# Empty places between the links of the ordered mixer's chains, and a second values block ahead of the second attention keys

## The chip, the cores and the metric

The kernel runs on one core of one Trainium2 chip. The metric is the device time of one execution in microseconds; the lower the better. TensorE is called PE here, VectorE DVE, ScalarE ACT, GpSimd POOL and SyncE SP, as the profile calls them.

## The reference

One decoder layer over 256 positions of width 2048: a feed-forward half step, a mixer of two groups of heads, a second feed-forward half step, each followed by a layer norm with a scaled residual.

```
x <- LN1(alpha*x + 0.5*SwiGLU_1(x))
x <- LN2(alpha*x + W_out [DiffAttn(x) || RWKV7(x)])
x <- LN3(alpha*x + 0.5*SwiGLU_2(x))
```

The mixer matters here. One projection `w_in` gives the columns of both kinds of heads. Differential attention has 8 heads with two softmaxes each: p = softmax(q1 k1) - lam * softmax(q2 k2), o = p v, then a norm over the head. RWKV7 has 16 heads of size 64, and its state goes from one position to the next:

```
sa    = einsum('bhvk,bhk->bhv', state, -kk_t)
state = state * w_t + sa * (kk_t * a_t) + v_t * k_t
y_t   = einsum('bhvk,bhk->bhv', state, r_t)
```

after a shift by one position, a decay w and a rate a from two low-rank products ("lora"), and a normalised kk. y goes through a group norm, gets a bonus from r, k and v, and is multiplied by a gate g. Both results go through `W_out`.

## The kernel before

**The weight stream.** Every weight comes from HBM once, in float32. A block of 512 columns takes 8 steps of 256 rows each. One step (`Stream.block`) loads 512 KB with a DMA on SP's queue (L130), ACT rounds it into `wh` (L140), DVE writes the rest, `wl` = raw - `wh` (L143), and PE forms two times six matmuls of 128x512: hi x wh (L150), hi x wl (L151), lo x wh (L152), for the first 128 positions of this step and for the second 128 of the step two back. In the mixer there are five pairs of `wh` and `wl`, so the pair of a step is used again five steps later, and three buffers for the raw weights.

**The chains as background.** At the end of each step `run_bg` goes over the generators that were spawned and lets each advance by one place: it calls `next` until the generator yields something other than 0. So `yield 0.6` (or any number but 0) ends a place, `yield 0` goes on in the same place, and `yield None` waits for a condition and asks again in the next place. `hold` skips a generator for some places. Below, place n is the n-th step after the one in which the lora block's results are turned (L575 for the first time).

**What the order is made of.** The mixer's part up to the last `stream.flush` runs under `manual_schedule` for PE: PE executes in the order in which the program is written. The order on DVE, ACT and POOL is set by a scheduler. Their instructions run in that order, so a DMA that ACT issues, or an operation that waits, holds up what is queued behind it there.

The blocks of `w_in` in this part: the lora block (8 steps), then twelve blocks of 8 steps: r1 (k, r, v of RWKV group 1), a1's q and k, r2's k and r, v1 (attention's first values), a2's q and k, r2's v, v2. When a block is finished, `chan_major` (L569 copies on ACT, L575 transposes on PE, one place later) or a copy hands it to the chains. Here r1, r2 are the two groups of eight RWKV heads (g = 0 and 1 in the code), a1, a2 the two groups of four attention heads.

**The RWKV chain of a group**, `rwkv_group`: L735 multiplies the lora result by its second matrix into the banks `pr` and `sm`, L739 puts a sigmoid on it (ACT), L743 sums the decays (DVE). When k is there, L749 to L752 prepare kk on DVE and ACT, L757 sums its squares over a head (PE), L758 to L774 scale everything on DVE and ACT. When r is there, L783 scales it; L793 forms the products of all positions of a chunk (PE, into `sm` and `pr`), L796 masks them into `Q` (DVE). Then `dU` and `U` go through HBM by DMAs from ACT's queue (L823, L826), L834 and L836 eliminate, 31 pairs of operations on DVE over 16 places, and the inverse goes back by more such DMAs (L840, L841 write `dY` and `dYT`, L848 and L852 read them). L860 and L871 finish the inverse; L811 turns `BK`; the four chunks c follow, links L890, L902 to L912, L921 and the output. After the last chunk L951 and L961 do the group norm, and L981 the gate. The second group waits with L793 until the first one's chunks are done ("chain").

**`rwkv_values`** turns v (L705, L712) and forms the bonus (`rk` at L699, L719).

**Attention**, `attn_heads`, two generators per group with two heads each: scores L1039 (PE, into `at` and `pr`), bias L1041 and maximum L1044, L1045 (DVE), exponentials L1049 (ACT), combination L1051 to L1055 (DVE), transposes L1060 and their copy L1062, product with v L1072, norm L1081 to L1096 (ACT, DVE and POOL), transposes L1100 and copy L1101.

Of the kernel before, what the change touches and what calls it, by code (L numbers as in the profile page):

```python
# [10 lines left out]
F32 = mybir.dt.float32  # L11
# [5 lines left out]
P = 128  # L17
D = 2048
S = 256
# [18 lines left out]
def build(tc, A, out):  # L38
# [58 lines left out]
    class Stream:  # L97
# [184 lines left out]

        def spawn(self, gen):
            self.bg.append(gen)

# [262 lines left out]
    def mix(mp, pq, C):  # L548
# [140 lines left out]
        def merge(x):  # L689
            return x.rearrange("p a c t -> p (a c) t")  # L690

        def rwkv_values(g, st):
            gr, prev = st["group"], st["prev"]
            while "fed" not in st or (prev is not None and "chain" not in prev):
                yield None
            vp, vv = gr.vp, gr.vv
            rk = t4("lw") if g == 0 else mp.tile([P, 4, S], F32, tag="vv", name=nm("rk"))
            for p in range(4):
                V.scalar_tensor_tensor(out=v4(rk)[:, p], in0=gr.rh[:, p], scalar=col(4, g, p), in1=gr.ka[:, p], op0=ALU.mult, op1=ALU.mult)  # L699
            SV = hp.tile([P, 4, 4, 2, 64], F32, tag="J1", name=nm("SV"))  # L700
            st["SV"] = SV
            for p in range(4):
                ps = bank(("pr", "sm")[p % 2], (P, 4, P))
                for c in range(4):
                    T.transpose(ps[:, c, :], vp[:, p, c * 64:c * 64 + P], ident)  # L705
                SC.copy(out=SV[64:128, p, :, 0, :], in_=ps[64:128, :, 0:64])
                SC.copy(out=SV[0:64, p, 0:3, 1, :], in_=ps[0:64, 1:4, 64:128])
                if p % 2 == 1:
                    yield 0.3
            ps = bank("pr", (P, 4, P))  # L710
            for p in range(4):
                T.transpose(ps[0:64, p, :], vv[:, p, 192:256], ident)  # L712
            SC.copy(out=SV[0:64, :, 3, 1, :], in_=ps[0:64, :, 64:128])
            st["turned"] = True
            yield 0.3
            for hf in range(2):
                ps = bank(("pr", "sm")[hf], (P, 2, S))
                for p in range(2):
                    T.matmul(ps[:, p, :], C["bones"], rk[:, 2 * hf + p, :], start=True, stop=True)  # L719
                V.tensor_tensor(out=vv[:, 2 * hf:2 * hf + 2, :], in0=ps, in1=vv[:, 2 * hf:2 * hf + 2, :], op=ALU.mult)  # L720
            yield 0.6
            st["values"] = True

        def rwkv_group(g, st):
# [5 lines left out]
            while "tw" not in lora:  # L730
                yield None
            for k in range(2):
                ps = [bank(t, (P, 2, S)) for t in ("pr", "sm")]
                for p in range(4):
                    T.matmul(ps[p // 2][:, p % 2, :], wa[:, p * P:(p + 1) * P], lora["tw"][:, k, :], start=True, stop=True)  # L735
                for p in range(4):
                    x = ps[p // 2][:, p % 2, :]
                    o, x = (tl[:, p, :], x) if k == 0 else (av[:, p], x.rearrange("p (c t) -> p c t", c=4))
                    SC.activation(out=o, in_=x, func=AF.Sigmoid, bias=col(k, g, p))  # L739
                yield 0.6  # L740
# [7 lines left out]
            for p in range(4):  # L748
                V.tensor_scalar(out=al[:, p], in0=ka[:, p], scalar1=col(2, g, p), scalar2=-1.0, op0=ALU.mult, op1=ALU.mult)  # L749
            SC.activation(out=v4(tl), in_=al, func=AF.Square)  # L750
            for p in range(4):
                V.tensor_scalar(out=be[:, p], in0=av[:, p], scalar1=-1.0, scalar2=col(3, g, p), op0=ALU.add, op1=ALU.mult)  # L752
# [9 lines left out]
            V.scalar_tensor_tensor(out=merge(ka), in0=merge(be), scalar=1.0, in1=merge(ka), op0=ALU.add, op1=ALU.mult)  # L762
            yield 1.1
            V.tensor_tensor(out=merge(al), in0=merge(al), in1=merge(v4(tl)), op=ALU.mult)
            yield 1.1

            SC.activation(out=tl, in_=cum, func=AF.Exp, scale=LDEC)
            SC.activation(out=cum, in_=cum, func=AF.Exp, scale=-LDEC)
            V.scalar_tensor_tensor(out=merge(av), in0=merge(av), scalar=-1.0, in1=merge(al), op0=ALU.mult, op1=ALU.mult)
            yield 1.1  # L770
# [12 lines left out]
            V.tensor_tensor(out=merge(rh), in0=merge(rh), in1=merge(v4(cum)), op=ALU.mult)  # L783
            yield 1.1
            while prev is not None and "chain" not in prev:
                yield None
# [13 lines left out]
            def transposed():  # L800
# [5 lines left out]
                for h in range(2):  # L806
                    for e in range(2):
                        r = slice(64 * e, 64 * e + 64)
                        ps = bank("sm", (P, 6, 64))
                        for i in range(6):  # L810
                            T.transpose(ps[:, i, :], BK[r, 2 * h + i // 3, i % 3, e:e + 2].rearrange("p a t -> p (a t)"), ident[r, r])  # L811
                        for p in range(2):
                            SC.copy(out=bt[2 * h + p][:, 0:3, e, :], in_=ps[:, 3 * p:3 * p + 3])
# [143 lines left out]
            for hf in range(2):  # L957
# [4 lines left out]
                SC.activation(out=merge(nrm[:, h2]), in_=merge(v4(ps)), func=AF.Ln, scale=1.0 / 64, bias=C["ge"])  # L962
                yield 0.6 * hf
            SC.activation(out=merge(nrm), in_=merge(nrm), func=AF.Exp, scale=-0.5)
            yield 0
# [7 lines left out]
            st["gate"] = True  # L973
            yield 0.6 * (1 - g)
            o = (hp, mp)[g].tile([P, 4, S], F32, tag=("H3", "vvd")[g], name=nm("og"))
# [25 lines left out]

        def attn_cols(g):
            st = {"q": qq[:, g]}

            def qkdone(tt, acc, n):
# [5 lines left out]
                def then():  # L1011
                    if n == "k":
                        st["left"] = 2
                        st["gens"] = [attn_heads(g, st, (i, i + 2)) for i in range(2)]
                        for i, x in enumerate(st["gens"]):
                            stream.spawn(x)
                            stream.hold[x] = i

                chan_major(acc, tt, [P] * 4, dst, then)

            stream.block(w_in, g * NB, NB, KX, x_lhs, lambda tt, acc: qkdone(tt, acc, "q"))
            stream.block(w_in, AW + g * NB, NB, KX, x_lhs, lambda tt, acc: qkdone(tt, acc, "k"))
            return st

        def attn_heads(g, st, heads):
            q, k = st["q"], st["k"]
            W = 3 * P
            spans = [slice(0, P), slice(P, W)]
            for h in heads:
# [23 lines left out]
                for qb in range(2):  # L1053
                    V.tensor_scalar(out=s[:, 0, spans[qb]], in0=s[:, 0, spans[qb]], scalar1=rr[:, qb, 0:1], scalar2=None, op0=ALU.mult)
                    V.scalar_tensor_tensor(out=s[:, 0, spans[qb]], in0=s[:, 1, spans[qb]], scalar=rr[:, qb, 1:2],  # L1055
                                           in1=s[:, 0, spans[qb]], op0=ALU.mult, op1=ALU.add)
                yield 0.6
                tr = bank("at", (P, 4, P))
# [6 lines left out]
                while "v" not in st:  # L1065
                    yield None
                if wait and heads[0] == 1:
                    yield 0.6
                vt = st["v"]
# [25 lines left out]
                for qb in range(2):  # L1095
                    V.tensor_scalar(out=ot[:, qb, :], in0=po[:, qb, :], scalar1=rs[:, 0, qb:qb + 1], scalar2=None, op0=ALU.mult)  # L1096
                yield 0.6
                tr = bank("at", (P, 4, P))
# [18 lines left out]
        attn_values(0, a1)  # L1117
        a2 = attn_cols(1)
        rwkv_cols(1, r2, (2,))
        attn_values(1, a2)  # L1120
# [137 lines left out]
```

## Time and profile before

| | |
|---|---|
| median of 3 runs | 1970.33 us (1967.61 to 1971.26) |
| the profiled execution's own time | 1970.74 us |
| its span in the trace | 1969.0 us |
| mean granted clock of TensorE | 0.983 |
| first FFN | up to about 706 us of the span |
| the mixer | about 706 to 1262 us |
| bytes read from HBM | 368.29 MB |

The profile is one execution, so its span (first to last instruction) and its own time are compared with each other, and the median of the runs with other medians. Where the text says "the mixer's window" it means 735 to 1131 us of the span, in which the chains named above run beside the stream. In the profile a row of a group gives how often an operation ran, its busy time, the mean ns of one, and the idle time of its engine just ahead of it with what ended it. A row of the table of waits gives which PE line waited for which instruction, how long in all, how often, and the longest.

### The profile page before, as it was taken

To read this page: it belongs to the slowest core of one execution; us is meant where nothing else is said; L and a number is where in the kernel's file an instruction comes from. 1 tells how busy PE (TensorE), PEld (TensorE's weight loads), DVE (VectorE), ACT (ScalarE), POOL (GpSimd) and SP (SyncE) were. 2 spreads that over 40 slices of the span, in tenths; PEclk is the share of its full clock that TensorE was granted. 3 is DMA by queue.
4 is the path that set the end of the run, shared out by engine and by line. 5 is a ranking of instruction groups with operands and counts; after the bars stand their busy time and mean duration, and the time that the engine had idled before them with its cause. 6 is when DMAs were issued, how large, how long until landed. Compare 5 with 4: busy or idle time off the path is not lost. (4 is left out here: it accounts for less than half of the span.)

```text
span 1969.0 us, 24893 instructions
## 1 busy us (share of the span) xinstructions
PE 1895.0 (96%) x9319; PEld 1554.9 (79%) x9319; DVE 1620.6 (82%) x1826; ACT 1094.9 (56%) x1376; POOL 73.0 (4%) x110
## 2 busy tenths in 40 slices
PE   9999999999999988889789999999999999999997
PEld 7788888888888877677667778788888888888886
DVE  7999988789998775586568676899999868899986
ACT  5656655556665545445444554366666555666652
POOL 0000101000000000000000000000000100000000
PEclk9999999999999999999899999999999999999999
DMA  8756676666666563445334546596556686556744
GB/s 298 247 201 223 192 240 225 223 210 219 204 201 207 163 193 107 139 137 152 97 110 145 150 138 206 191 309 221 182 193 203 226 276 214 182 193 215 226 164 133
DMA packets 207320, 381.72 MB, mean 194 GB/s; under 512 B 23530, under 2 KB 25648, under 8 KB 206944
## 3 DMA queue, kind: packets, MB, share of 16 engines
q1 hardware_dynamic: 182928, 350.53, 54.2%
q0 software_dynamic: 6832, 15.32, 2.9%
q10 hardware_dynamic: 17440, 14.29, 2.5%
q8 instruction: 73, 1.20, 0.2%
q14 instruction: 47, 0.39, 0.1%
HBM read 368.29 MB, written 11.80 MB: 193 GB/s over the span
## 5 line engine op out<-in xcount | busy, mean ns | idle before, releaser
L140 ACT CAST wh<-raw 128x1024 fp32r<-128x1024 f32 (+2 forms) x833 | 853.1, 1047 | 660.5 <-PE acc L152 437.0
L143 DVE TENSOR_TENSOR wl<-raw,wh 128x1024 fp32r<-128x1024 f32 (+2 forms) x833 | 983.4, 1213 | 230.8 <-ACT wh L140 226.3
L150 PE MATMUL acc<-wh,xh 128*128 128x512 f32 (+1 forms) x1552 | 612.0, 400 | 1.8 <-ACT xh L87 1.0
L151 PE MATMUL acc<-wl,xh 128*128 128x512 f32 (+1 forms) x1552 | 608.5, 393 | 2.1 <-DVE wl L143 2.0
L152 PE MATMUL acc<-wh,xl 128*128 128x512 f32 (+1 forms) x1552 | 607.4, 392 | 0.4 <-DVE xl L88 0.4
L150 PEld LDWEIGHTS acc<-wh,xh 128*128 128x128 f32 x1552 | 295.6, 191 | 65.6 <-issue 2.4
L152 PEld LDWEIGHTS acc<-wh,xl 128*128 128x128 f32 x1552 | 294.9, 190 | 62.3 <-DVE xl L88 1.1
L151 PEld LDWEIGHTS acc<-wl,xh 128*128 128x128 f32 x1552 | 295.4, 190 | 61.4 <-DVE wl L143 3.4
L221 DVE TENSOR_TENSOR raw<-raw,raw 128x2048 f32<-128x2048 f32 x112 | 255.8, 2284 | 2.3 <-DMA raw<-in_ffn_w_up_dram 1.0
L151 PE MATMUL acc<-wl,hh 128*128 128x512 f32 x544 | 212.0, 390 | 0.0
L152 PE MATMUL acc<-wh,hh 128*128 128x512 f32 x544 | 211.4, 389 | 0.0
L150 PE MATMUL acc<-wh,hh 128*128 128x512 f32 x544 | 210.9, 390 | 0.0
L150 PE MATMUL acc<-wh,s 128*128 128x512 f32 x448 | 174.9, 390 | 2.1 <-ACT wh L140 1.1
L152 PE MATMUL acc<-wh,s 128*128 128x512 f32 x448 | 174.6, 390 | 0.0
L151 PE MATMUL acc<-wl,s 128*128 128x512 f32 x448 | 174.4, 389 | 0.0
L150 PEld LDWEIGHTS acc<-wh,hh 128*128 128x128 f32 x544 | 102.1, 188 | 21.7 <-ACT wh L140 0.4
L152 PEld LDWEIGHTS acc<-wh,hh 128*128 128x128 f32 x544 | 102.1, 188 | 21.1
L151 PEld LDWEIGHTS acc<-wl,hh 128*128 128x128 f32 x544 | 102.1, 188 | 20.9
L150 PEld LDWEIGHTS acc<-wh,s 128*128 128x128 f32 x448 | 84.1, 188 | 20.3 <-ACT wh L140 1.5
L152 PEld LDWEIGHTS acc<-wh,s 128*128 128x128 f32 x448 | 84.1, 188 | 17.5
L151 PEld LDWEIGHTS acc<-wl,s 128*128 128x128 f32 x448 | 84.1, 188 | 17.4
L234 ACT COPY acc<-acc 128x512 f32<-128x512 f32 x28 | 16.0, 571 | 51.3 <-PE acc L152 47.5
(287 smaller groups left out, 1105.9 us busy)
## 6 DMA issues: line engine op xcount, KB each, us to landing
raw<-in_ffn_w_up_dram SPq DMA_DIRECT2D x176, 512.0 KB, 5.4
raw<-in_ffn_w_down_dram SPq DMA_DIRECT2D x176, 512.0 KB, 5.2
raw<-in_ffn_w_gate_dram SPq DMA_DIRECT2D x175, 512.0 KB, 4.6
raw<-in_w_in_dram SPq DMA_DIRECT2D x96, 512.0 KB, 3.6
raw<-in_w_out_dram SPq DMA_DIRECT2D x32, 512.0 KB, 3.8
sd<-s POOLq DMA_DIRECT2D x16, 256.0 KB, 4.0
s<-sd POOLq DMA_DIRECT2D x16, 256.0 KB, 4.9
xs<-y ACTq DMA_DIRECT2D x16, 256.0 KB, 2.7
```

Of the source, the lines that this page charges most:

```text
L140: SC.copy(out=wh[:, c, :w], in_=raw[:, c, :w])
L143: self.cut = V.tensor_tensor(out=wl[:, c, :w], in0=raw[:, c, :w], in1=wh[:, c, :w].bitcast(F32), op=ALU.subtract).ins
L150: T.matmul(a, hi, wh[:, j, :w], start=first and j == 0, stop=False, skip_group_check=True)
L151: T.matmul(a, hi, wl[:, j, :w], start=False, stop=False, skip_group_check=True)
L152: i = T.matmul(a, lo, wh[:, j, :w], start=False, stop=last and j == 1, skip_group_check=True)
L221: V.tensor_tensor(out=out, in0=x, in1=y, op=ALU.subtract)
L234: SC.copy(out=u, in_=a)
```

## The change

`rest(n)` is a generator that yields n places. The change puts it into the chains and moves some of their instructions:

- RWKV group: two empty places ahead of L735 in the first group; three ahead of L752; after L762 one in the first group (as before) and two in the second; one more ahead of L769 in the second group; three after L783 instead of one.
- The second group's L793 waits for the first group's norm ("normed") instead of the end of its chunks ("chain"), and the first group's gate (L981) waits until the second group's L793 are issued ("fed").
- L811 of the second group uses the bank `pr` for half of its transposes.
- Values: three empty places ahead of L705, one more ahead of L719; `rk` is formed after L712.
- Attention: an empty place ahead of the first head; the second pair of heads is held two places instead of one; in the first group two places instead of one ahead of L1060 and L1100; after the wait for v four places in the second pair of the first group (one in the second group). The first group's heads stand first in the background list.
- The second RWKV group's v block comes ahead of the second attention keys block, and behind the queries block.

```
+        def rest(n):
+            for i in range(n):
+                yield 0.6
...
-            rk = t4("lw") if g == 0 else mp.tile([P, 4, S], F32, tag="vv", name=nm("rk"))
-            for p in range(4):
-                V.scalar_tensor_tensor(out=v4(rk)[:, p], in0=gr.rh[:, p], scalar=col(4, g, p), in1=gr.ka[:, p], op0=ALU.mult, op1=ALU.mult)
+            yield from rest(3)
...
             while "tw" not in lora:
                 yield None
+            yield from rest(2 * (1 - g))
...
             SC.activation(out=v4(tl), in_=al, func=AF.Square)
+            yield from rest(3)
...
             V.tensor_tensor(out=merge(rh), in0=merge(rh), in1=merge(v4(cum)), op=ALU.mult)
-            yield 1.1
-            while prev is not None and "chain" not in prev:
+            yield from rest(3)
+            while prev is not None and "normed" not in prev:
                 yield None
...
-                        ps = bank("sm", (P, 6, 64))
+                        ps = bank(("sm", "pr")[e * g], (P, 6, 64))
...
+            st["normed"] = True
...
-            yield 0.6 * (1 - g)
+            while g == 0 and "fed" not in st["next"]:
+                yield None
...
-                            stream.spawn(x)
-                            stream.hold[x] = i
+                            stream.spawn(x, (i, None)[g])
+                            stream.hold[x] = 2 * i
...
             stream.block(w_in, g * NB, NB, KX, x_lhs, lambda tt, acc: qkdone(tt, acc, "q"))
+            between()
             stream.block(w_in, AW + g * NB, NB, KX, x_lhs, lambda tt, acc: qkdone(tt, acc, "k"))
...
-                yield 0.6
+                yield from rest(2 - g)
                 tr = bank("at", (P, 4, P))
...
-                if wait and heads[0] == 1:
-                    yield 0.6
+                if wait:
+                    yield from rest((1 + 3 * (1 - g)) * heads[0])
...
-        a2 = attn_cols(1)
-        rwkv_cols(1, r2, (2,))
+        a2 = attn_cols(1, lambda: rwkv_cols(1, r2, (2,)))
```

The changed kernel has a few more lines, so its lines count higher: L735 is L742 there, L752 is L760, L783 is L792, L793 is L802, L796 is L805, L834 and L836 are L843 and L845, L840 and L841 are L849 and L850, L848 and L852 are L857 and L861, L985 is L996, L1009 is L1020, L1049 is L1062, L1101 is L1114.

On the engines the instructions move as follows. First PE at place 25, where the second group's lora product stands. Before, the transposes of a block (L575) come ahead of it, and the stream follows:

```order
L150 MATMUL acc_6441<-wh_6559,xh_5804 128x512
L151 MATMUL acc_6441<-wl_6560,xh_5804 128x512
L152 MATMUL acc_6441<-wh_6559,xl_5805 128x512
L575 MATMUL tr_6643<-ident,tm_6599 128x128 x4
L735 MATMUL pr_6659<-tw,qq 128x256 x2
L735 MATMUL sm_6660<-tw,qq 128x256 x2
L150 MATMUL acc_6630<-wh_6671,xh_5678 128x512
L151 MATMUL acc_6630<-wl_6672,xh_5678 128x512
```

In the changed kernel the same place (L802 is L793 of before, L742 is L735):

```order
L802 MATMUL sm_6635<-AR_5962,BK_5963 128x128
L802 MATMUL pr_6636<-AR_5962,BK_5963 128x128
L742 MATMUL pr_6647<-tw,qq 128x256 x2
L742 MATMUL sm_6648<-tw,qq 128x256 x2
L150 MATMUL acc_6570<-wh_6659,xh_5689 128x512
L151 MATMUL acc_6570<-wl_6660,xh_5689 128x512
```

The first group's products have moved from places 19 to 22 to places 24 to 27, and stand right ahead of the second group's lora product, in the same two banks.

Second, ACT where the first group's inverse goes out and comes back (`dY`, `dYT`, `TT`, `YT`). Before:

```order
L1009 COPY qq<-tr_6998 128x4x128
L840 DMA dY_6608<-Y_6616 64x1024
L841 DMA dYT_6609<-U_6614 32x1024
L140 CAST wh_7084<-raw_7082 128x1024
L848 DMA TT_7158<-dY_6608 32x16x32 x4
L852 DMA YT_7164<-dYT_6609 32x16x32
L140 CAST wh_7108<-raw_7106 128x1024
L852 DMA YT_7164<-dYT_6609 32x16x32
L140 CAST wh_7134<-raw_7132 128x1024
```

In the changed kernel:

```order
L140 CAST wh_7306<-raw_7304 128x1024
L849 DMA dY_6759<-Y_6767 64x1024
L850 DMA dYT_6760<-U_6765 32x1024
L857 DMA TT_7294<-dY_6759 32x16x32 x3
L1062 ACT_TABLE_LOAD
L1062 ACTIVATE s_7209,ssum_7211<-s_7209,mx_7210 128x128 x2
L1062 ACTIVATE s_7209,ssum_7211<-s_7209,mx_7210 128x256 x2
L857 DMA TT_7294<-dY_6759 32x16x32
L861 DMA YT_7300<-dYT_6760 32x16x32 x2
L140 CAST wh_7327<-raw_7325 128x1024
```

No cast of the weight stream stands between the issues any more, and the exponentials of the first attention head (L1062) stand among them.

Third, DVE at the second group's elimination. Before, its first operations are spread between subtractions of the stream (L143):

```order
L143 TENSOR_TENSOR wl_8240<-raw_8237,wh_8239 128x1024
L834 TENSOR_TENSOR itmp_8192<-U_8168,Y_8170 64x31
L143 TENSOR_TENSOR wl_8288<-raw_8285,wh_8287 128x1024
L836 TENSOR_TENSOR Y_8170<-Y_8170,itmp_8192 64x31
L834 TENSOR_TENSOR itmp_8195<-U_8168,Y_8170 64x60
L836 TENSOR_TENSOR Y_8170<-Y_8170,itmp_8195 64x30x2
L143 TENSOR_TENSOR wl_8326<-raw_8323,wh_8325 128x1024
L834 TENSOR_TENSOR itmp_8217<-U_8168,Y_8170 64x87
```

In the changed kernel (L843 and L845 are L834 and L836; `og` is the first group's gated output, `qq` a finished head of attention):

```order
L143 TENSOR_TENSOR wl_8493<-raw_8490,wh_8492 128x1024
L843 TENSOR_TENSOR itmp_8402<-U_8352,Y_8354 64x60
L996 TENSOR_TENSOR og_8392<-BK_5963,sm_8393 128x512
L845 TENSOR_TENSOR Y_8354<-Y_8354,itmp_8402 64x30x2
L843 TENSOR_TENSOR itmp_8435<-U_8352,Y_8354 64x87
L845 TENSOR_TENSOR Y_8354<-Y_8354,itmp_8435 64x29x3
L843 TENSOR_TENSOR itmp_8438<-U_8352,Y_8354 64x112
L845 TENSOR_TENSOR Y_8354<-Y_8354,itmp_8438 64x28x4
L843 TENSOR_TENSOR itmp_8484<-U_8352,Y_8354 64x135
L1114 TENSOR_SCALAR qq<-at_8425,ng 128x256
L845 TENSOR_TENSOR Y_8354<-Y_8354,itmp_8484 64x27x5
L843 TENSOR_TENSOR itmp_8487<-U_8352,Y_8354 64x156
```

More of the elimination's operations stand in a row between two subtractions than before.

More of the change, by code (lines that the diff above doesn't have):

```diff
@@ L281, in flush, with spawn @@
                 self.puts.pop(0)[1]()
-        def spawn(self, gen):
-            self.bg.append(gen)
+        def spawn(self, gen, at=None):
+            self.bg.insert(len(self.bg) if at is None else at, gen)
         def put(self, f):
@@ L714, in rwkv_values @@
             st["turned"] = True
+            rk = t4("lw") if g == 0 else mp.tile([P, 4, S], F32, tag="vv", name=nm("rk"))
+            for p in range(4):
+                V.scalar_tensor_tensor(out=v4(rk)[:, p], in0=gr.rh[:, p], scalar=col(4, g, p), in1=gr.ka[:, p], op0=ALU.mult, op1=ALU.mult)
             yield 0.3
+            yield 0.6
             for hf in range(2):
@@ L762, in rwkv_group @@
             V.scalar_tensor_tensor(out=merge(ka), in0=merge(be), scalar=1.0, in1=merge(ka), op0=ALU.add, op1=ALU.mult)
-            yield 1.1
+            yield from rest(1 + g)
             V.tensor_tensor(out=merge(al), in0=merge(al), in1=merge(v4(tl)), op=ALU.mult)
@@ L768, in rwkv_group @@
             SC.activation(out=cum, in_=cum, func=AF.Exp, scale=-LDEC)
+            yield from rest(g)
             V.scalar_tensor_tensor(out=merge(av), in0=merge(av), scalar=-1.0, in1=merge(al), op0=ALU.mult, op1=ALU.mult)
@@ L783, in rwkv_group @@
             V.tensor_tensor(out=merge(rh), in0=merge(rh), in1=merge(v4(cum)), op=ALU.mult)
-            yield 1.1
-            while prev is not None and "chain" not in prev:
+            yield from rest(3)
+            while prev is not None and "normed" not in prev:
                 yield None
@@ L1000, in attn_values, with attn_cols @@
             stream.block(w_in, 2 * AW + g * NB, NB, KX, x_lhs, vdone)
-        def attn_cols(g):
+        def attn_cols(g, between=lambda: None):
             st = {"q": qq[:, g]}
@@ L1025, in attn_heads @@
         def attn_heads(g, st, heads):
+            yield 0.6
             q, k = st["q"], st["k"]
@@ L1096, in attn_heads @@
                     V.tensor_scalar(out=ot[:, qb, :], in0=po[:, qb, :], scalar1=rs[:, 0, qb:qb + 1], scalar2=None, op0=ALU.mult)
-                yield 0.6
+                yield from rest(2 - g)
                 tr = bank("at", (P, 4, P))
```

## The prediction

> **What bounds the kernel now.** I read the page first. Its rows for the span and for the engines put TensorE (PE) far ahead of the rest:
>
> ```profile
> span 1969.0 us, 24893 instructions
> PE 1895.0 (96%) x9319; PEld 1554.9 (79%) x9319; DVE 1620.6 (82%) x1826; ACT 1094.9 (56%) x1376; POOL 73.0 (4%) x110
> ```
>
> The mean hides stages, so next the table by stretches; its columns are length, then PE, PEld, DVE, ACT and POOL busy, the granted clock, the DMA share and GB/s. The first row lies in the first FFN, the second is the ordered mixer up to the 1131st us, the third is what follows it:
>
> ```profile
> 100.00:700.00 600.00, 599.51 (x2685) 496.69 (x2684) 527.25 (x477) 352.85 (x388) 26.78 (x40) 1.00 0.63 207
> 735.00:1131.00 396.00, 350.26 (x2104) 279.44 (x2105) 256.09 (x477) 194.58 (x327) 6.81 (x7) 0.94 0.45 131
> 1131.00:1250.00 119.00, 117.60 (x792) 95.18 (x791) 83.46 (x154) 58.41 (x112) 5.70 (x7) 1.00 0.54 176
> ```
>
> The FFN has no idle PE to win. The ordered mixer has 396.00 - 350.26 = 45.7 us of it, and its clock stands at 0.94; behind it another 1.4 us lie idle. What PE waits for in the second stretch, from the table of waits (in all, times, longest):
>
> ```profile
> PE pr L757 <- ACT tl L750: 9.9, 2, 5.3
> PE pr L705 <- DVE vv L591: 9.0, 2, 6.7
> PE sm L793 <- DVE AR L783: 5.7, 1, 5.7
> PE sm L890 <- DVE SV L921: 5.2, 1, 5.2
> PE at L1100 <- DVE ot L1096: 4.5, 2, 4.2
> PE pr L735 <- ACT tw L615: 3.7, 1, 3.7
> PE sm L981 <- DVE Q L796: 2.3, 1, 2.3
> PE acc L151 <- DVE wl L143: 1.5, 2, 0.8
> ```
>
> Nearly all of it is a link of a chain that stands in PE's row before its input is ready, not the weight stream (the last row, 1.5 us). The timeline around the third row shows how a link costs (start, length, engine, line):
>
> ```profile
> 800.29 0.39 PE L150 MATMUL acc<-wh,xh 128*128 128x512 f32 x1
> 800.52 0.39 PE L151 MATMUL acc<-wl,xh 128*128 128x512 f32 x1
> ...
> 802.80 1.23 DVE L143 TENSOR_TENSOR wl<-raw,wh 128x1024 fp32r<-128x1024 f32 x1 [0.45 <-ACT wh L140]
> ...
> 805.52 1.23 DVE L783 TENSOR_TENSOR AR<-AR,cum 128x1024 f32<-128x1024 f32 x1
> ...
> 806.80 2.08 PE L793 MATMUL sm<-AR,BK 64*128 64x128 f32 x16 [5.66 <-DVE AR L783]
> ...
> 810.25 0.63 PE L150 MATMUL acc<-wh,xh 128*128 128x512 f32 x1
> 810.68 0.63 PE L151 MATMUL acc<-wl,xh 128*128 128x512 f32 x1
> ```
>
> DVE serves weights and link in turn, PE stands for 5.66 us, and after it the matmuls come every 0.43 us instead of every 0.23. The windows of half clock that follow such gaps, three of the nine and the sum of all nine:
>
> ```profile
> 805.79:812.62 6.83, 5.82 (x25) 4.83 (x26) 3.93 (x8) 0.00 (x0) 0.00 (x0) 0.50 0.17 62
> 996.94:1000.35 3.41, 3.41 (x21) 2.54 (x19) 3.41 (x7) 0.00 (x0) 0.00 (x0) 0.50 0.51 157
> 1116.40:1119.81 3.41, 3.08 (x11) 2.54 (x12) 1.68 (x4) 1.52 (x3) 0.00 (x0) 0.50 0.89 304
> sum 51.21, PE 40.87 PEld 32.50 DVE 32.30 ACT 11.08 POOL 1.01; mean PE 4.54 PEld 3.61 DVE 3.59 ACT 1.23 POOL 0.11
> ```
>
> PE works 40.87 us in them; at full clock that work takes 40.87 x 0.23/0.43 = 21.9, so the low clock costs 19.0 us. All that an ideal order could win is 45.7 + 1.4 + 19.0 = **66.1 us**.
>
> **The change, part by part.** One place of the stream is 12 matmuls of 0.23 us, 2.76 us. Three empty places are 8.3 us, more than the longest links in the rows above (6.7, 5.7, 5.3). So the rests ahead of L757 (both groups), L705 (both) and L793 of the first group, and two ahead of the first L735 (5.5 us against 3.7), take these gaps: 9.9 + 9.0 + 5.7 + 3.7 = 28.3 us. The cover is weight work that PE has to do anyhow, so an empty place costs nothing itself; it pushes the link later, and the chains end before the stream does. The gate of the first group waits for the second group's L793 to be issued, so L981 no longer stands right behind the DVE work of L796 (2.3). The 3.9 us that the eight rows don't hold are small waits of attention; its heads get an empty first place and a second one ahead of L1060 and L1100 (first group), which covers them. All this I take as gone. The rests cannot help a weight step that is late; what is new is where links now stand close. Five such places, each with the rows that price it, first the groups of the second stretch (last columns: busy, mean ns of one, idle before):
>
> ```profile
> L143 DVE TENSOR_TENSOR wl<-raw,wh 128x1024 fp32r<-128x1024 f32 x91 | 110.7, 1219 | 70.1 <-ACT wh L140 69.5
> L834 DVE TENSOR_TENSOR itmp<-U,Y 64x31 f32<-64x31 f32 (+15 forms) x62 | 20.5, 331 | 9.5 <-DMA U<-dU 8.5
> L836 DVE TENSOR_TENSOR Y<-Y,itmp 64x31 f32<-64x31 f32 (+15 forms) x62 | 20.5, 330 | 1.1
> L140 ACT CAST wh<-raw 128x1024 fp32r<-128x1024 f32 x91 | 95.1, 1047 | 129.1 <-PE acc L152 104.2 <-issue 17.4 <-DMA raw<-in_w_in_dram 3.9
> L796 DVE TENSOR_TENSOR Q<-sm,maskq 128x512 f32<-128x512 f32 x12 | 7.9, 684 | 1.5 <-PE sm L793 1.5
> L773 DVE TENSOR_TENSOR BK<-BK,tl 64x1024 f32<-64x1024 f32 x2 | 2.4, 1206 | 0.0
> L569 ACT COPY tm<-acc 128x512 f32<-128x512 f32 x20 | 11.7, 586 | 24.1 <-PE acc L152 18.1 <-issue 3.7 <-DVE Q L796 2.3
> L1049 ACT ACTIVATE s<-s,mx 128x128 f32<-128x128 f32 (+1 forms) x24 | 10.6, 448 | 5.7 <-DVE mx L1045 5.7
> L902 ACT COPY SV<-sm 64x256 f32<-64x256 f32 x4 | 1.5, 368 | 0.1
> L1049 ACT ACT_TABLE_LOAD x1 | 1.3, 1283 | 0.0
> ```
>
> *A, place 25.* The second group's L735 keeps its place while the first group's L793 moves right ahead of it, and it writes the banks that L793 has just filled. L796 must empty them (0.68 us), and on DVE a weight subtraction now stands in between, which waits for L569 (0.59) and the cast (1.05) and takes 1.22 itself: 2.9 us from the end of L793, little of it covered; I take **2.9** (0 if the subtraction is early, 4 if its buffer is late too).
>
> *B, place 47.* ACT issues DMAs in its row. dY's issue, then L848, which waits for dY to land, then the exponentials of the first heads with their table load stand between two casts, where before only L848 and L852 stood between a cast and the next:
>
> ```profile
> DMA to landing us min/median/max: 3.8/3.8/3.9
> ...
> 874.97 0.48 ACTq L840 DMA_DIRECT2D dY<-Y  x1
> ...
> 876.14 0.32 ACTq L841 DMA_DIRECT2D dYT<-U  x1
> ...
> 878.91 1.95 ACTq L848 DMA_DIRECT2D TT<-dY  x4
> ...
> 880.90 0.80 ACTq L852 DMA_DIRECT2D YT<-dYT  x1
> ```
>
> The first row is dY's landing. Cast 1.05, issues 0.8, landing 3.8, L848 1.95, table 1.28, four exponentials 1.8, L852 0.8 to 1.3, the next cast 1.05 and its subtraction 1.22 make 14 us, and some 2 to 3 for waits on DVE and for hand-overs, as the trace has 0.45 us between a cast and its subtraction above. Buffers cover five places, 13.8 us. I take **3.0** (0 to 5).
>
> *C, places 70 to 78.* Two costs. L793 of the second group waits for a bank that L1041 empties behind a subtraction: 1.5. The larger is L1100 of the first group's later heads at place 78. Between it and the place where its attention values are formed, DVE now has 7 subtractions (8.5 us), 34 of the elimination's L834 and L836 (11.2 us) and 24 small operations at an estimated 0.22 us each, two thirds of an L834 (5.3): 25.0 us against six places, 16.6, and about 1 us of links. That is **7.2**. The elimination comes in one block because U, which comes back by DMA, lands later against the stream than before; before, PE waited for L1100 4.5 us for the same reason. C is 8.7 (4 to 12; the lower end is the wait of before, the upper is if the two small transfers land late).
>
> *D, places 58 and 59.* L890 of the chain loses its stall of 5.2 us, since DVE is less full there, but the next links stand behind L771 and L773 (1.2 us each, of which about 0.95 is left when PE comes) and behind L902, which queues after a cast and its subtraction (1.9). **2.9** (1 to 5).
>
> *E.* One weight step is late behind L783 at place 19, 0.7 us, as the two of 1.5 us are now; 1.0 for the rest.
>
> Sum: 2.9 + 3.0 + 8.7 + 2.9 + 1.7 = 19.2 us idle. A window costs its length x (1 - 0.23/0.43), so 1.6 for 3.41 us and 3.2 for 6.83: A 1.6, B 1.6, C 2.7 (it may share its window with work), D 0.8 (an even chance): 6.7.
>
> Whether A, B and D cost clock at all is the one point where a rule bears. Here gaps of this size did: the two short windows above begin behind these waits.
>
> ```profile
> 995.85 1.13 PE L981 MATMUL sm<-gs,g 128*128 128x256 f32 x4 [2.32 <-DVE Q L796]
> ```
>
> The Trainium skill, page "TensorE: Matmul & The Clock Gate", Part 1 ("The HAM clock gate"), has the clock fall after at least one idle window of some 3.4 us. By that page A, B and D would cost no clock, and the sum would come out 4 us lower, 1926. The trace does not agree: 2.32 us were enough for a window of 3.41 us at 0.50, so the sum goes by the trace.
>
> Gain: 66.1 - 19.2 - 6.7 = 40.2 us. The profiled execution took 1970.74 us, 1.7 over its span, and 0.4 more than the median of 1970.33; the cost around the span stays. 1970.33 - 40.2 = **1930 us**. With A to E halved (9.6 + 3.4) it is 1917; with 1.75 times (33.6 + 11.7) 1950.
>
> **The rivals.**
>
> *Covered.* The new stalls aren't there: DVE is 65% busy in the second stretch, 256.09 of 396.00, and ACT 49%, so the scheduler's queues may run ahead of what I count. Then some 4 us of idle remain: 1970.3 - 66.1 + 4 = 1908. Against it: every gap of before stood behind a DVE queue that was full just there.
>
> *The change doesn't do what it says.* The rests move the consumers, but the producers are set by a scheduler, and move back with them, so that half of the gaps stay. Then half of 66.1 - 25.9 is won, 20 us: 1950. For it: the weight subtractions fill DVE between the links whatever the order. Against it: in PE's order the links stand three places further from what feeds them.
>
> *Slower.* DVE becomes the bound at half clock. If late subtractions at places 24 to 32 and 72 to 96 leave a gap in each place, the clock stays at 0.50 throughout them, and a place takes 12 x 0.43 = 5.2 us, 2.4 more. Over all of some 35 places that is 84 us against a gain of 66: 1988. It decides from 28 places on. Against it: after each of the three windows above the clock came back within 6.83 us, though DVE was feeding weights and chains there as well; and a gap in every place needs DVE work of over 2.76 us per place, where the second stretch has 256.09 us in 396.00.
>
> **How the numbers follow.** A measurement can tell about 0.2%, 4 us, from no change. Forecast 0.62, covered 0.18, half 0.15, slower 0.03, the rest (0.02) between. Faster by over 0.2% hold forecast, covered and half: 0.95; the same 0.02, slower 0.03. The range goes from the covered case, 1908, to the bound of the costs and the half case, 1950; the outer parts of these cases and the slower one are left out.
>
> **What would show it.** The idle of PE in the mixer's window falls from 45.7 to about 19 us, and the half-clock windows from nine to five or so. The waits for L757, L705, L783 and tw vanish from the table. New rows are L735 waiting for L796 (about 2.9), a weight step after the exponentials that waits for a cast on ACT (3.0), and L1100 behind L1096 (7.2). If L1100's row stays under 3 us, C is wrong; if those for L757 or L705 stay at 9, the half case holds; if the granted clock of the mixer falls below 0.94, the slower one.

## The result and the profile after

The changed kernel took 1919.29 us (median of 4 runs, 1918.37 to 1920.22); the kernel before, beside it, 1970.8 (4 runs). The ratio is 0.9734, with a 95% interval from 0.9709 to 0.976. The forecast was 1930 in a range of 1908 to 1950. The profiled execution took 1918.37 us, 52.4 less than that of before.

First the page after, the rows for the span and the engines:

```profile
span 1916.6 us, 24892 instructions
PE 1875.8 (98%) x9319; PEld 1543.8 (81%) x9319; DVE 1620.1 (85%) x1826; ACT 1093.1 (57%) x1376; POOL 74.3 (4%) x110
```

DVE and ACT do the same work as before; PE is busy 19 us less with the same 9319 matmuls, so they ran faster. The whole mixer in one stretch, first before and then after (columns as in the prediction):

```profile
716.00:1250.00 534.00, 483.80 (x2995) 388.64 (x2994) 353.58 (x652) 263.49 (x453) 12.52 (x14) 0.95 0.48 144
```

```profile
714.00:1198.00 484.00, 466.50 (x2998) 378.79 (x2996) 353.45 (x652) 262.62 (x454) 13.44 (x14) 0.99 0.53 159
811.15:814.56 3.41, 2.95 (x7) 2.41 (x8) 1.24 (x3) 0.83 (x2) 0.00 (x0) 0.50 0.52 154
1022.78:1029.61 6.83, 5.12 (x15) 4.27 (x16) 6.49 (x17) 1.06 (x2) 0.00 (x0) 0.50 0.45 145
```

PE's idle time in the mixer fell from 534.00 - 483.80 = 50.2 us to 484.00 - 466.50 = 17.5. Of the nine stretches at half clock (40.87 us of PE work) two are left (8.07); by the pitches of 0.23 and 0.43 us their cost fell from 19.0 to 3.8 us. (One more, from 712 to 716 us, belongs to the layer norm ahead of this stretch; the trace of before has none there.) Idle 32.7 and clock 15.2 make 47.9 of the 50 us between the two stretches. What PE still waits for, the table of waits of the changed kernel:

```profile
PE at L1113 <- DVE ot L1109: 4.2, 1, 4.2
PE acc L151 <- DVE wl L143: 3.5, 2, 2.0
PE pr L742 <- DVE Q L805: 2.5, 1, 2.5
PE sm L921 <- DVE SV L910: 1.4, 1, 1.4
PE sm L909 <- DVE Rs L901: 1.3, 1, 1.3
PE sm L802 <- DVE Q L805: 1.1, 1, 1.1
PE pr L802 <- DVE s L1054: 1.0, 1, 1.0
PE at L1052 <- ACT qq L1020: 0.9, 1, 0.9
PE sm L742 <- DVE Q L805: 0.4, 1, 0.4
```

In the lines of before, L1113 is L1100, L742 is L735, L921 is L912, L909 is L900, L802 is L793, L1052 is L1039, L805 is L796 and L1054 is L1041. The rows of before for the sums of squares (L757), the values (L705), L783, tw and the gate are gone.

### The profile page after: what moved, and what is told of

The parts are those of the page before. It is cut to its first block, busy times and chain, and to the rows that moved or that the text cites. A ratio compares the mean times of both kernels' runs of the same rounds, so it can differ in the third digit from the quotient of the medians.

```text
span 1916.6 us, 24892 instructions
## 1 busy us (share of the span) xinstructions
PE 1875.8 (98%) x9319; PEld 1543.8 (81%) x9319; DVE 1620.1 (85%) x1826; ACT 1093.1 (57%) x1376; POOL 74.3 (4%) x110
## 5 line engine op out<-in xcount | busy, mean ns | idle before, releaser
L143 DVE TENSOR_TENSOR wl<-raw,wh 128x1024 fp32r<-128x1024 f32 (+2 forms) x833 | 983.3, 1212 | 200.6 <-ACT wh L140 195.5
L151 PE MATMUL acc<-wl,xh 128*128 128x512 f32 (+1 forms) x1552 | 604.1, 390 | 3.7 <-DVE wl L143 3.5
L151 PEld LDWEIGHTS acc<-wl,xh 128*128 128x128 f32 x1552 | 292.9, 189 | 62.2 <-DVE wl L143 5.2
L151 PE MATMUL acc<-wl,hh 128*128 128x512 f32 x544 | 212.0, 390 | 0.0
L151 PE MATMUL acc<-wl,s 128*128 128x512 f32 x448 | 174.4, 389 | 0.0
L151 PEld LDWEIGHTS acc<-wl,hh 128*128 128x128 f32 x544 | 102.1, 188 | 21.1
L152 PEld LDWEIGHTS acc<-wh,s 128*128 128x128 f32 x448 | 84.1, 188 | 17.5
L151 PEld LDWEIGHTS acc<-wl,s 128*128 128x128 f32 x448 | 84.1, 188 | 17.5
```

The source lines that it names most:

```text
L143: self.cut = V.tensor_tensor(out=wl[:, c, :w], in0=raw[:, c, :w], in1=wh[:, c, :w].bitcast(F32), op=ALU.subtract).ins
L151: T.matmul(a, hi, wl[:, j, :w], start=False, stop=False, skip_group_check=True)
L152: i = T.matmul(a, lo, wh[:, j, :w], start=False, stop=last and j == 1, skip_group_check=True)
```

## The experiments

The theory: a link that stands in PE's row behind its producer's queue waits, and each empty place takes 2.76 us off that wait; a long wait brings one or two windows of half clock (3.41 us each) with it, and they go too. The rivals: the order of the blocks or attention's places make the gain; or the scheduler moves the producers along, so that empty places do little. All ratios are to the kernel before on the same chip, with 95% intervals.

**chain_rests.** The kernel before with the chain's part of the change alone:

```
+            yield from rest(3)            # values, ahead of L705
...
+            yield 0.6                     # ahead of L719, where rk is formed now
...
+            yield from rest(2 * (1 - g))  # ahead of L735
...
+            yield from rest(3)            # ahead of L752
...
-            yield 1.1                     # after L783
+            yield from rest(3)
```

The second group's extra places after L762 and ahead of L769 are not in it.

> The kernel before with the rests of the RWKV chain and of the values alone (ahead of L735, L752, L705 and L719, two more after L783, and rk formed later); attention, the gates and the order of the blocks stay as before. Theory (each rest takes its own link's wait and the half clock behind it): the waits for L757, L705, L793 of the first group and L735, 28.3 us, and some 14 us of low clock go, the wait of the second L735 behind L793 (2.5 us and a short window) comes: some 36 us less than before, 1934. Rival (the order of the blocks and attention's rests carry the larger half): 20 us less, 1950.

Measured: 0.9762 (0.9749 to 0.9775), 1925.43 us. These rests alone win some 47 of the 52 us, more than the 36 that I expected. Their trace has no wait for the first lora product, the sums of squares, L783 or the values left. Two waits that the expectation left out are gone or nearly so as well, the 5.2 us of L890 and the 4.2 of L1100 (0.6 is left there).

**others_only.** The opposite, the changed kernel without the rests of the chain and the values:

```
-            yield from rest(3)
...
-            yield 0.6
...
-            yield from rest(2 * (1 - g))
...
-            yield from rest(3)
...
-            yield from rest(1 + g)
+            yield 1.1
...
-            yield from rest(g)
...
-            yield from rest(3)
+            yield 1.1
```

`rk` is formed ahead of L705 again, as before.

> The changed kernel without the rests of the RWKV chain and the values (the opposite of chain_rests): what is left are attention's places, the gates, the bank of L820 and the order of the blocks. Theory (the chain's rests carry the gain): the waits for the first lora product, the sums of squares, L802 and L707 stand as before, and only what chain_rests lacked is won, about 5 us: 1 to 8 us faster than before, 0.996 to 0.9995 of it. Rival (the parts overlap, each alone gets most of it): 20 us faster or more, 0.99 or less.

Measured: 0.9952 (0.994 to 0.9964), 1962.86 us: 9.5 us of gain, somewhat more than the 1 to 8 expected. Its table of waits holds the rows of before (L709 is the values' L705, L761 is L757, L797 is L793, L894 is L890, L739 is L735):

```profile
PE pr L709 <- DVE vv L591: 11.4, 2, 6.2
PE pr L761 <- ACT tl L754: 9.9, 2, 5.3
PE sm L797 <- DVE AR L787: 6.2, 1, 6.2
PE sm L894 <- DVE SV L925: 5.2, 1, 5.2
PE pr L739 <- ACT tw L615: 3.6, 1, 3.6
```

47 and 9.5 add up to 56 against 52, so the two parts hardly overlap. The rival that another part carries the gain falls. What the second group's extra places after L762 and ahead of L769 do by themselves is not shown, as neither kernel has them.

**old_order.** The changed kernel with the v block of the second RWKV group behind the second keys:

```
-        a2 = attn_cols(1, lambda: rwkv_cols(1, r2, (2,)))
+        a2 = attn_cols(1)
+        rwkv_cols(1, r2, (2,))
```

> The changed kernel with the second RWKV group's v block behind the second attention keys again. Theory (rests carry the gain): the values' links move from places 85 and 86 to 93 and 94 but keep their three empty places, so no wait for L707 (L705 of before) comes back: within 3 us of the changed kernel, 1917 to 1922. Rival (the order of the blocks is what makes room): over 8 us slower, 1927 or more, with waits for L707 or L1052 after the 1030th us.

Measured: 0.9733 (0.9719 to 0.9746). The order of the blocks is worth nothing that can be measured, with the rests in place. In others_only, where the rests are missing, the earlier v block met a wait of 5.2 us at its L709 (11.4 - 6.2 in the rows above), where the later one met 2.3 in the kernel before (9.0 - 6.7).

**no_attn_rests.** The changed kernel with attention's places as before:

```
-            yield 0.6
             q, k = st["q"], st["k"]
...
-                yield from rest(2 - g)
+                yield 0.6
...
-                if wait:
-                    yield from rest((1 + 3 * (1 - g)) * heads[0])
+                if wait and heads[0] == 1:
+                    yield 0.6
...
-                            stream.hold[x] = 2 * i
+                            stream.hold[x] = i
```

> The changed kernel with attention's places as before (no empty first place, one place instead of two ahead of L1073 and L1113, hold of one place, short wait after v). Theory: the small waits of attention come back (L1060, L1072, L1100 of before: 2.4 us with those that were below 1), and the wait for L1113 in the first group grows by up to one place of 2.8 us, with one more half-clock window: 4 to 10 us slower than the changed kernel, 1923 to 1929. Rival (heads and the elimination collide more because the heads are spread): as fast or faster, 1915 to 1920.

Measured: 0.9738 (0.9725 to 0.9751), against 0.9734 and 0.9735 for the changed kernel, some 0.7 us: no difference that can be told. The theory expected 4 to 10 and falls; the rival had the time right. Its trace has the waits in other places: L1112 (the L1113 of the changed kernel) waits 2.8 and 0.5 instead of 4.2, and the product with v waits 3.5. The waits were exchanged, not added.

**old_gates.** The changed kernel with the gates and the bank as before:

```
-            while prev is not None and "normed" not in prev:
+            while prev is not None and "chain" not in prev:
...
-            while g == 0 and "fed" not in st["next"]:
-                yield None
+            yield 0.6 * (1 - g)
...
-                        ps = bank(("sm", "pr")[e * g], (P, 6, 64))
+                        ps = bank("sm", (P, 6, 64))
```

> The changed kernel with the gates as before: the second group's L802 waits for the end of the first one's chunks, the first group's gate (L992) comes one place after the norm, and L820 of the second group uses one bank. Neither the order of the blocks nor attention's places made a difference of 2 us in the runs before, so if chain_rests lacks 5 us by one part alone, it is this one. Theory: L992 at places 66 and 67 stands where DVE is full of norm and scores and waits 0.7 to 2.5 us, as in chain_rests, with a window of half clock, and L820 waits twice 0.6 us: 3 to 7 us slower than the changed kernel, 0.975 to 0.977 of before. Rival (no part alone carries it; each gap only comes when two of them meet): within 1.5 us, 0.9728 to 0.9743.

Measured: 0.9781 (0.9768 to 0.9794), 1929.03 us: 9 us slower than the changed kernel, more than the 3 to 7 expected. The wait that the theory had at L992 did not come; L802 waits behind the gate instead. Three rows that the changed kernel doesn't have, or not so long:

```profile
PE sm L802 <- DVE og L995: 2.5, 2, 2.0
...
PE pr L707 <- ACT SV L709: 1.7, 1, 1.7
PE sm L820 <- ACT BT L822: 1.4, 2, 0.8
```

They are 5.6 us together, 4.5 more than the 1.1 of L802 that they replace, and behind L802's wait the trace has another window of half clock, 1.6 us. That makes 6 of the 9; the others are not placed (two more windows lie behind weight steps that are late in the changed kernel too). So of what lies outside the chain's rests, the gates are the part that counts; the second bank, which went with them here, is in the row of L820 (1.4 us). The prediction had given the gates 2.3 us.

**fix_a.** The changed kernel with term A taken away; the second group's L742 stands behind all of the first group's L802:

```
-            yield from rest(2 * (1 - g))
+            yield from rest(2 + 2 * g)
```

> The changed kernel with four empty places ahead of the second group's first L742, so that it stands at places 28 and 29, behind all four of the first group's L802 instead of between them. Theory (term A: L742 waits for L805 to empty the banks that L802 has just filled): the waits of 0.4 and 2.5 us go and the window of half clock at 811 us with them (3.4 us at 0.50, 1.6 us): 4 to 5 us faster than the changed kernel, 1914.5 to 1915.5. Rival (DVE is simply behind there, and whatever stands next waits as long): the wait moves to the next link or to L151, and the time stays within 1.5 us of 1919.

Measured: 0.9703 (0.9689 to 0.9716), against 0.9734 and 0.9735 for the changed kernel: 6 us. The waits of 2.5 and 0.4 us and the window of half clock behind them are gone from the trace; only 0.2 us for L742 is left. The rival, that the next link would wait instead, falls. The 6 us are not told apart from the 4 to 5 expected, as each ratio is known to 0.0013, 2.6 us.

**after_again.** The changed kernel again, as a base.

> The changed kernel once more, as the base on the same chip for the three beside it: 0.9734 of the kernel before, as in its first timing, within 0.002.

Measured: 0.9735 (0.9721 to 0.9748).

**dose0 and dose1.** On fix_a, the first group's empty places between L792 and L802: none, and one, instead of three:

```
-            yield from rest(3)
+            yield from rest(3 * g)      # dose0
+            yield from rest(1 + 2 * g)  # dose1
```

> The kernel of fix_a without the three empty places between L792 and L802 in the first group, so that L802 stands at place 21. In the trace of the changed kernel L792 ends 4.2 us ahead of L802's start at place 24. Theory (a place covers 2.76 us of a link that does not move with it): L802 waits 3 x 2.76 - 4.2, some 4 us, and a window of half clock follows, 1.6 to 3.2 us: 5.5 to 7.5 us slower than fix_a. Rival (the scheduler moves L792 and what feeds it with its reader): no wait for L802 over 1.5 us, within 1.5 us of fix_a.

> The same with one empty place, as the kernel before had, so that L802 stands at place 22. Theory: a wait of 2 x 2.76 - 4.2 = 1.3 us; that is too short for a window of half clock by what the runs so far show (no gap under 1.9 us was followed by one): 1 to 2 us slower than fix_a. Rival (it is the empty places after L792 that carry the gain at L793 of before): the wait of 5.7 us and its 6.83 us of half clock are back, 8 to 9 us slower.

Measured: 0.9775 (0.9762 to 0.9788) and 0.9754 (0.9741 to 0.9767); fix_a has 0.9703. The waits themselves, from the timelines of dose0 and of dose1:

```profile
800.10 1.23 PE L802 MATMUL sm<-AR,BK 64*128 64x128 f32 x8 [4.05 <-DVE AR L792]
```

```profile
798.35 1.23 DVE L792 TENSOR_TENSOR AR<-AR,cum 128x1024 f32<-128x1024 f32 x1
799.63 0.60 PE L802 MATMUL sm<-AR,BK 64*128 64x128 f32 x6 [1.34 <-DVE praw L660]
```

The second row names L660, a memset of 0.06 us that ended beside L792; L792 itself ends at 799.58, just ahead of L802. Some 4 and 1.3 us were expected, from 3 and 2 places of 2.76 us less the 4.2 us of spare time: 4.05 and 1.34 came. The producers do not move with their readers, and a place is worth its 2.76 us. But the totals are 14 and 10 us by the ratios, not 5.5 to 7.5 and 1 to 2. Between the profiled executions they are 10.5 and 8.8: PE's idle time in the mixer is 5.5 and 5.4 us longer than in fix_a, and the low clock costs 5.9 and 3.4 us more. Of that clock 1.6 us is a window behind the late weight step at place 19, which waits 2.0 us in all three traces, but in fix_a without a window; that part owes nothing to the doses. The rest lies behind L802: the chain starts two to three places earlier, and its links meet other DVE work. In dose1 the L899 at place 52 (L890 of before) waits as it did before the change, with a window of half clock behind it:

```profile
941.13 1.22 DVE L143 TENSOR_TENSOR wl<-raw,wh 128x1024 fp32r<-128x1024 f32 x1
942.28 0.17 DVE L786 COPY PC<-qq 128x16 f32<-128x16 f32 x1
942.36 1.20 DVE L787 TENSOR_TENSOR AR<-AR,qq 128x1008 f32<-128x1008 f32 x1
943.48 0.86 DVE L930 TENSOR_TENSOR SV<-St,PC 64x256 f32<-64x256 f32 x2
944.03 1.27 PE L899 MATMUL sm<-SV,Q 128*64 128x64 f32 x14 [4.30 <-DVE SV L930]
```

L930, which L899 needs, stands behind the second group's L778 to L787. So a rest acts twice: on its own link, and by where it puts all links behind it against the other chains' work. That second part is what the theory left out.

**fix_ac.** fix_a with one more place ahead of L1113 in the first group:

```
-                yield from rest(2 - g)
+                yield from rest(3 - g)
```

> The kernel of fix_a with a third empty place ahead of the first attention group's L1113 (term C). Theory (L1113 waits 4.2 to 4.4 us because DVE is that far behind with the elimination, and 2.8 us more of matmuls cover most of it): the wait falls to about 1.5 us and the 6.83 us of half clock at 1021 us go: 5 to 6 us faster than fix_a, 0.967 to 0.968 of the kernel before. Rival (the DVE queue falls behind as much as the place is moved): within 1.5 us of fix_a, 0.9695 to 0.971.

Measured: 0.9675 (0.9662 to 0.9688), 1906.88 us: 5.5 us less than fix_a by the ratios, and 12 less than the changed kernel. The wait for L1113 is gone from its table of waits, and no window of half clock is left from 716 us to the stretch's end (a wait of 1.2 us before L1085, the product with v, is new); its stretch now reads:

```profile
714.00:1188.00 474.00, 465.28 (x3008) 377.60 (x3007) 353.39 (x653) 262.89 (x455) 12.70 (x14) 1.00 0.55 163
```

8.7 us idle, full clock. This version beats both kernels.

**fix_ac_pool.** fix_ac with one DVE operation of the first group on POOL:

```
-            V.tensor_tensor(out=merge(av[64:128]), in0=merge(av[64:128]), ...
+            (G if g == 0 else V).tensor_tensor(out=merge(av[64:128]), in0=merge(av[64:128]), ...
```

> The kernel of fix_ac with the first group's L783 on POOL instead of DVE (term E: the weight subtraction at place 19 is 2.0 us late in all runs, behind L778 to L787 on DVE, 1.2 us each). Theory: DVE has 1.2 us less there, the wait falls to some 0.8 us, and no window of half clock can follow it: 1 to 3 us faster than fix_ac, 0.966 to 0.967 of before. Rival (an operation on POOL holds DVE up, or L792's chain waits for POOL): as fast as fix_ac or up to 3 us slower, 0.9675 to 0.969.

Measured: 0.9681 (0.9666 to 0.9695), against 0.9675 for fix_ac: no gain. From its timeline:

```profile
783.04 3.08 POOL L783 TENSOR_TENSOR BK<-BK,tl 64x1024 f32<-64x1024 f32 x1 [71.09 <-DVE BK L778]
783.79 3.42 DVE L780 TENSOR_TENSOR BK<-BK,tl 128x1024 f32<-128x1024 f32 x1
...
790.73 0.50 PE L151 MATMUL acc<-wl,xh 128*128 128x512 f32 x1 [2.84 <-DVE wl L143]
```

DVE's L780 takes 3.42 us beside POOL's L783; in fix_ac it took 1.22. The late subtraction became later, 2.84 us instead of 2.02. The theory fell here; the rival was right.

## Why the prediction was right

**What could be won.** I had 66.1 us; the two stretches above give 50.2 + 19.0 = 69.2. The window that I read began at 735 us, inside the first gap, which had begun at 732.5, and cut 2.5 us off it.

**That the chain's rests carry the gain** and that empty places cost nothing themselves: right, shown by chain_rests and others_only. The reason given was slightly off in one place. I counted three new places after L783, where before had one already; two were added, and three with those ahead of L752 moved L802 from place 19 to 24. dose0 and dose1 show that L802 had 4.2 us to spare there, so one place fewer would have done for its own link.

**A**, 2.9 us with 1.6 of clock: measured 2.5 + 0.4, and a window of 3.41 us with 2.95 of PE work, 1.4. fix_a shows the cause, and its 6 us agree with these 4.3 within the noise. The idle time is the firm part: in the trace of after_again L742 waits the same 2.5 us and no window follows.

**B**, 3.0 us with 1.6 of clock: the wait at place 47 was 1.4 us (1.7 in the trace of after_again), on the weight steps that I had named, with a window in the second trace only. The size was within its bounds, but half.

**C**, 8.7 us with 2.7 of clock: the two waits of L802 came to 2.1 (1.5 forecast) and that for L1113 to 4.2 (7.2 forecast). This is the largest error among the terms. DVE's row was counted right: from the first elimination operation at 998.8 us to L1109 at 1024.0 there are 34 of them, 7 subtractions and 22 small operations, 25.2 us where I had 25.0. The two ends, and what PE waited, from the timeline:

```profile
998.78 0.20 DVE L843 TENSOR_TENSOR itmp<-U,Y 64x31 f32<-64x31 f32 x1 [2.64 <-DMA U<-dU]
...
1024.00 0.59 DVE L1109 TENSOR_SCALAR ot<-at,ars 128x128 f32<-128x128 f32 x2
...
1024.49 0.66 PE L1113 MATMUL at<-ident,ot 128*128 128x128 f32 x2 [4.20 <-DVE ot L1109]
```

What failed is the other side: "against six places, 16.6, and about 1 us of links". From 998.78 to 1024.49 are 25.7 us; less PE's waits of 4.2 and 0.9 that leaves 20.6 us of work, the 16.6 of the six places and some 4 of other links: the attention heads' own matmuls take about 2 of them, and the first group's gate (L992 and L995), which now stands there, about 1.6. U also landed sooner than before, where it took 5.3 to 5.7 us; the view of its DMA's line in the changed kernel gives, for both groups:

```profile
DMA to landing us min/median/max: 3.5/4.2/4.9
```

So the reason given for the block of elimination work was wrong too. U does not come later against the stream: before, the second group's elimination began 8.4 us ahead of this L1100 (1023.79 against 1032.24), now it begins 25.7 us ahead of it. fix_ac shows that the wait is DVE's lag and that one more place covers it.

**D**, 2.9 us: 1.3 + 1.4 came, but no window of half clock, as the even chance allowed.

**E**, 0.7 us: 2.0, with three, one or no place behind L792 alike; 0.8 in others_only, where the chain's rests are missing ahead of L765 too. The rests put L778 to L787 where two weight steps are due. The 1.0 for the rest was 2.1, of which L1052 is 0.9.

Together 17.5 us idle against 19.2, and 3.8 of low clock against 6.7; of the five or so stretches at half clock two came. The idle sum is nearer than its terms, by luck: B and C were 4.0 us too high, E and the rest 2.4 too low. Between the profiled executions the gain is 52.4 us, 12.2 more than the 40.2 of the forecast: 3.1 (what could be won), 1.7 (idle) and 2.9 (clock) make 7.7 of it. Of the others, the two executions differ by 2.0 us ahead of the stretches (716 against 714 us) without a cause in the change, and some 2.5 us stay open.

**The rivals.** "Covered", at 1908, did not happen: the stalls A, C, D and E were all there. That the measured time lies as near to 1908 as to 1930 is because they are a little smaller, not because they are missing. "The change doesn't do what it says" is refuted by the doses: producers stayed, and with no, one and three empty places the reader waited 4.05 us, 1.34 us and not at all. "Slower" did not happen: in the changed kernel's 484 us the clock is at 0.99.

**The gates**, which I gave 2.3 us, are worth 9 with the second bank (old_gates). That is more than the whole 5 us that chain_rests lacks; how the other parts make up for it is not shown. That attention's places cover its waits was wrong: without them nothing is lost.

## What to carry to other kernels

Where PE executes a fixed order and another engine feeds it, read the table of waits by link: a wait of some us that ends with a link's producer is cured by standing the link that many steps of streaming work later, and each step is worth its own length. But count what the shift does to every link behind it, because it lands on other chains' work: the doses cost 1.3 and 4 us at their own link and 10 and 14 us in all. Then look for a link that writes a bank just filled, and separate it; that was worth some 6 us here (fix_a), as much as one more place for the longest wait left (5.5 us in fix_ac).

## What the runs showed of the hardware

**The half clock goes by windows, not by gaps.** All changes of the granted clock inside the mixers of a trace lie on one grid of 3.41 us. The same wait at the same instruction (2.0 us for L151 at place 19) was followed by half clock in some runs and not in others. old_order, where the whole wait lies in one cell of the grid, and the changed kernel, where 0.14 us of it reach into the next; for each the cell with the wait and the one after it:

```profile
785.58:789.00 3.42, 1.41 (x6) 0.86 (x5) 3.39 (x5) 1.13 (x2) 0.00 (x0) 1.00 0.00 1
789.00:792.41 3.41, 3.41 (x9) 2.63 (x8) 3.25 (x6) 0.51 (x1) 0.00 (x0) 0.50 0.82 252
```

```profile
783.84:787.25 3.41, 1.52 (x7) 0.94 (x5) 3.38 (x4) 1.79 (x3) 0.00 (x0) 1.00 0.14 52
787.25:790.66 3.41, 3.26 (x14) 2.68 (x15) 3.26 (x5) 0.51 (x1) 0.00 (x0) 1.00 0.63 187
```

2.0 us of idle PE in one cell cost the clock of the next, 1.9 us did not. In the thirteen traces here, all 40 cells at full clock with 1.99 us or more of idle time, from 716 us to the end of the layer norm that closes the mixer, were followed by half clock; of some twenty with 1.5 to 1.9 us ahead of that layer norm two were. A wait of 2.79 us that lay half in each of two cells (no_attn_rests, before L1112) cost no clock. What PE does in the rest of the cell seems to count too, though no run isolates it: in the layer norm, where it does transposes, 1.55 us were enough (though 1.63 in old_gates was not), and in fix_ac_pool a cell with 1.0 us of idle time, 64 matmuls of 32x32 and three transposes was followed by half clock:

```profile
885.28:888.69 3.41, 2.40 (x70) 1.88 (x70) 3.41 (x8) 1.22 (x2) 0.00 (x0) 1.00 0.03 8
```

So the prediction's rows, which showed windows behind 2.3 us, were read rightly, but whether a wait of 2 to 3 us costs clock is a matter of where it falls. The Trainium skill, "TensorE: Matmul & The Clock Gate", Part 1, calls the window free-running, and the grid agrees with that. That the clock falls after at least one idle window does not fit: a cell with 1.41 us of work in 3.42 was enough.

**POOL slows DVE.** An operation on two operands took 3.42 us on DVE beside one of 3.08 us on POOL, against 1.22 without it (fix_ac_pool). It ended 1.09 us after POOL's (787.21 against 786.12 us), about its own length, as if it had stood until POOL was done; this is one case. The Trainium skill, "GPSIMD Engine Reference", section 1, has POOL share its SBUF interfaces with DVE, and the two contend when DVE's instruction has two inputs in SBUF; these numbers agree.
